# Moving the last tile's projection and key scores beside the gate stage, and spreading its top-k decoding over the expert blocks

## The chip, the core and the metric

The kernel runs on one core of one Trainium2 chip. The metric is the device time of one execution in microseconds (us), lower being better; before the change three executions took 2179.04, 2199.63 and 2200.12 us, with a median of 2199.63. The five engines are named as the profile names them: PE multiplies matrices, DVE and ACT work elementwise on 128 partitions, POOL does elementwise work and issues the indirect DMAs (the gathers), and SP issues the other DMAs, in order, from one queue.

## The reference

One layer of a hybrid decoder: a norm and an input projection, RWKV-7 time mixing and sliding-window attention side by side, an output projection with a residual, and then a PEER layer, to which the change belongs. The prompt has 512 tokens (four tiles of 128), the sample group has 32. Cut to what matters:

```python
def peer(h, lp):                       # 8 heads, 128 keys per half, top 16
    q = (hb @ w_query).reshape(PEER_BLOCK, PEER_HEADS, 2, D_HALF)
    s = jnp.einsum('thcd,cnd->thcn', q, sub_keys)
    s1, i1 = lax.top_k(s[:, :, 0], PEER_TOPK)
    s2, i2 = lax.top_k(s[:, :, 1], PEER_TOPK)
    cand, cidx = ...                   # the 16 x 16 sums, and i1 * 128 + i2
    top, sel = lax.top_k(cand, PEER_TOPK)
    idx = jnp.take_along_axis(cidx, sel, axis=-1)      # 128 experts of a token
    gate = jax.nn.softmax(top, axis=-1)
    act = jax.nn.gelu(jnp.einsum('td,tkd->tk', hb, eu[idx])) * gate
    return jnp.einsum('tk,tkd->td', act, ev[idx])
```

`expert_u` and `expert_v` have 16,384 rows of 1024 float32 each.

## The kernel before

The program is a straight line per engine; a scheduler orders each engine's instructions as the code emits them, by priorities and estimated durations, and every engine then works through its own list in that order.

It has these stages. The front (to about 1110 us) does the projection, the mixing, the attention and the first part of the PEER layer. The experts of the two middle prompt tiles are computed **densely**: the gates of their 256 tokens are spread into a table of 128 x 128 experts, and a loop of 128 blocks multiplies all experts, one block of 128 rows at a time. Those of the first tile, the sample group and the last tile (tile 3) are computed **sparsely**: POOL gathers each token's expert rows with an indirect DMA into a tile `gat`, DVE takes a dot product (`gat<-gat,h` or `gat<-gat,lx`) or adds a weighted row (`x<-gat,act,x`). There are 128 u rows and 128 v rows for a tile, and 32 of each for the sample group. "Rows" of this kind are issued by `beside(n)`, which adds n to a budget and issues one gather with its use per unit; what it takes them from is the list `side`, first in first out. `RATE_G` and `RATE_D` are the budgets of a group of the gates and of a block of the loop.

After the front comes the **gate stage**: two calls of `gates()` (L1387 to L1404) of 16 groups of 8 tokens. In each group DVE compares two one-hot tables (`uH<-vL,aH`, `uL<-vL,aH`), ACT multiplies six of eight by the gate (L1398) and DVE two, PE forms eight 128 x 128 outer products (L1401), and ACT copies them out, to a staging tile `uv` that SP writes to the DRAM tile `gscr` (first call, `stage`), or to `gA` and `gB` (second call, `keep`).

In the **loop** a block loads one block of each table into a tile of tag `uv` (five buffers, `UV`), transposes the u block on PE (L1446), splits both into two fp32r parts (`uH`, `uL`, `vH`, `vL`), multiplies (L1460 to L1463), applies GELU and the gates (`w<-w,gl`, `w<-w,gA`), splits the activation (`aH`, `aL`), and adds into four accumulators (L1477 to L1479). `vL` is a subtraction on POOL (L1453).

The generator `late()` (L1505 to L1551) does tile 3's part of the PEER layer up to its expert numbers: output projection (`w_out`, four steps, PE L1522), norm, transposes, then eight steps of `w_query` (L1544), each product copied (`lq`, L1546), multiplied by the keys (`skT`, L1547) and copied into scores (`lsc`, L1548), and after every second step `two_heads`, which decodes two heads' scores by top-16 searches (`MAX`, `MAX_INDEX`, `MATCH_REPLACE` and small operations on DVE, the `l...` tiles). Only after all eight heads are decoded does it append tile 3's rows to `side`. The loop steps the generator twice a block (`LATE`). The weights of a step are loaded where the step is.

The output stage (L1587 to L1603) adds the accumulators, norms and writes; `beside(1000)` issues whatever rows are left.

Tile pools are stretches of SBUF or PSUM. Where a pool is opened on the bytes of pools that were closed, its first users wait: with the default for every user of the closed pools, with `reuse_waits="tile"` each tile only for the users of what lay on its own bytes.

Of the kernel before, what the change touches and what calls it, by code (L numbers as in the profile page):

```python
# [11 lines left out]
F32 = mybir.dt.float32  # L12
# [5 lines left out]
PSUM = bass.MemoryType.PSUM  # L18
# [16 lines left out]
UV = 5  # L35
AHEAD = 280
RATE_G = 0.8
RATE_D = 3.0
# [75 lines left out]
def hymba_step(ctx, tc, x_prompt, x_sample, cache_k, cache_v, state_wkv, state_shift, meta, norm1_g, w_in, mu, w0,  # L114
# [28 lines left out]
    sscr = dr.tile([32, 16, 128], F32, name="sscr")  # L143
    yscr = dr.tile([128, 8, 128], F32, name="yscr")
# [825 lines left out]
    def two_heads(sc, dst, tile_):  # L970

# [4 lines left out]
        for j in range(4):  # L976
            top16(sc[:, j, :], vals[:, j // 2, j % 2, :], idx[:, j // 2, j % 2, :])
        idf = idx.bitcast(F32)
# [10 lines left out]
        for h in range(2):  # L989
            top16(cand[:, h, :], top[:, h, :], sel[:, h, :])  # L990
        pf = sm()
# [13 lines left out]
        G.tensor_tensor(d1[:, :, 1:16], idf[:, :, 0, 1:16], idf[:, :, 0, 0:15], OP.subtract)  # L1005
        full = [128, 2, 16, 16]
        res = dst[0:2] if len(dst) == 3 else [tile_("res", [128, 32]) for _ in range(2)]
        for r, tab, pos, op, val in ((res[0], first, pf, OP.is_le, d1), (res[1], iota16, bf, OP.is_equal, idf[:, :, 1, :])):
# [3 lines left out]
            V.tensor_reduce(r.rearrange("p (h k) -> p h k", h=2), eq, AX.X, OP.add)  # L1012
        if len(dst) == 2:
            V.scalar_tensor_tensor(dst[0], res[0], 128.0, res[1], OP.mult, OP.add)
# [265 lines left out]
    sb = fr.enter_context(tc.tile_pool(name="sb", bufs=1))  # L1280
    pp = fr.enter_context(tc.tile_pool(name="pp", bufs=1, space=PSUM))
# [98 lines left out]
    def gates(its, sel, ps, put):  # L1380
# [7 lines left out]
        for n, t8 in enumerate(range(0, 128, 8)):  # L1388
# [4 lines left out]
            for q0 in (0, 4):  # L1393
# [8 lines left out]
                put(t8 + q0, p)  # L1402
            with tc.issue_after(marks[-1]):
                beside(RATE_G)  # L1404
# [3 lines left out]
    dn = ctx.enter_context(tc.tile_pool(name="dn", bufs=1))  # L1408
    dp = ctx.enter_context(tc.tile_pool(name="dp", bufs=1, space=PSUM))
# [98 lines left out]
    def late():  # L1508
# [5 lines left out]
        def weights_of(w, n):  # L1514
            wt = dt_("uv", UV, [128, 8, 256])
            DM.dma_start(wt, w[0][:, 256 * n:256 * n + 256].rearrange("(k p) c -> p k c", p=128))
            return wt
        for n in range(4):
            wt = weights_of(w_out, n)
# [17 lines left out]
        for g in range(4):  # L1537
            sc = dt_("lsc", 1, [128, 4, 128])
            for j0 in (0, 2):
                wt = weights_of(w_query, 2 * g + j0 // 2)  # L1540
# [9 lines left out]
            two_heads(sc, [x[:, 32 * g:32 * g + 32] for x in pl1], late_tile)  # L1550
        side.append(tile_experts(3, *pl1, x2))  # L1551
# [8 lines left out]
    gates(its, sels[1], dps, keep)  # L1560
    gl = {}
# [13 lines left out]
    for j in range(128):  # L1575
# [7 lines left out]
        for _ in range(LATE):  # L1583
            next(more, None)
        with tc.issue_after(mark), tc.issue_after(sub):
            beside(RATE_D)
# [45 lines left out]
```

## Time and profile before

| | |
|---|---|
| Runs before (us) | 2179.04, 2199.63, 2200.12; median 2199.63 |
| Profiled execution | 2204.76 us; its span 2203.0 us |
| Busy, share of the span | PE 83%, DVE 77%, POOL 57%, ACT 39% |
| Front | 0 to about 1110 us |
| Gate stage | 1120 to about 1240 us |
| Loop, first to last `aL` | 1245.6 to 2180.3 us |
| After the last block's `aL` | 22.8 us |

All times in the profile are us from the start of the profiled span. The program is the same in each execution; the profiled one lies 5 us above the median of the runs. A row of a timeline is one instruction, or several alike that follow each other ("x6"), with its start and its duration; square brackets give the idle time of the engine before it, and what released it. A row of groups sums the instructions of one line and form. Matmuls are pipelined, and their ends are modelled, so that their starts say more than their durations.

### The profile page before, as it was taken

The page shows a single profiled execution, that of the slowest core. Times are in us where ns is not written, and L with a number is a line of the kernel's source. Part 1 is how long each engine was busy: PE and PEld are TensorE (multiplying, and loading weights), DVE is VectorE, ACT ScalarE, POOL GpSimd, SP SyncE. Part 2 cuts the span into 40 slices and gives each one's busy share as a digit, 9 for nine tenths or more (in the row PEclk, how much of TensorE's full clock was granted, in tenths as well). Part 3 has the DMA queues.
Part 4 walks back from the last instruction along what each step waited for, and adds up shares of the span by engine and source line. Part 5 has one row for each costly group of instructions (what it writes and reads, how often), then busy time and mean ns, then how long its engine had stood idle before and what let it go on. Part 6 is the DMA issues. An engine that isn't in the chain of part 4 may idle for free.

```text
span 2203.0 us, 37197 instructions
## 1 busy us (share of the span) xinstructions
PE 1839.1 (83%) x13915; PEld 1716.0 (78%) x13915; DVE 1690.4 (77%) x3393; ACT 867.3 (39%) x1963; POOL 1249.2 (57%) x963
## 2 busy tenths in 40 slices
PE   5899975585759868996547897899999999999996
PEld 5888974473647747886446787899999999999995
DVE  5543436788788788799989879997778787787887
ACT  6554422211224313323169634334444444444443
POOL 0110103878784676565624546867667776767774
PEclk9999996556755659898778999999999999999998
DMA  7532473687786789996757887799899999999995
GB/s 222 157 101 84 122 191 102 208 288 248 230 273 199 231 273 318 285 317 222 243 163 242 299 313 239 270 326 340 334 330 331 342 326 336 335 325 343 325 330 178
DMA packets 310154, 569.51 MB, mean 259 GB/s; under 512 B 32787, under 2 KB 194565, under 8 KB 309830
## 3 DMA queue, kind: packets, MB, share of 16 engines
q0 software_dynamic: 84048, 305.70, 39.7%
q1 hardware_dynamic: 225926, 261.43, 36.6%
q8 instruction: 110, 1.80, 0.3%
q14 instruction: 70, 0.57, 0.1%
HBM read 543.07 MB, written 24.60 MB: 258 GB/s over the span
## 4 chain that ended last, share of the span: by engine, by line
PE 51%; DVE 22%; DMA 10%; issue 9%; POOL 5%; ACT 3%; SPq 0%; DVEq 0%; POOLq 0%; ACTq 0%
DVE gat L126 5%; PE acc L1478 5%; PE w L1460 5%; PE w L1461 5%; PE w L1463 5%; PE acc L1479 5%; PE acc L1477 5%; PE w L1446 4%; POOL gat L1032 4%; DVE x L126 4%; PE pD L218 3%; DMA gat<-in_expert_v_dram,ei 3%; PE ps L218 2%; DMA wst<-in_w_query_dram 2%; DMA gat<-in_expert_u_dram,ei 2%
## 5 line engine op out<-in xcount | busy, mean ns | idle before, releaser
L126 DVE SCALAR_TENSOR_TENSOR x<-gat,act,x 128x1024 f32<-128x1024 f32 x287 | 427.9, 1491 | 24.7 <-DMA gat<-in_expert_v_dram,ei 23.4
L1032 POOL DMA_INDIRECT gat<-in_expert_u_dram,ei x256 | 343.0, 1340 | 158.8 <-DVE pre L126 75.7
L1032 POOL DMA_INDIRECT gat<-in_expert_v_dram,ei x256 | 294.4, 1150 | 193.6 <-DVE x L126 73.1
L1453 POOL TENSOR_TENSOR vL<-uv,vH 128x1024 fp32r<-128x1024 f32 x128 | 322.5, 2519 | 56.1 <-ACT vH L1452 54.3
L1478 PE MATMUL acc<-aL,vH 128*128 128x256 f32 x1024 | 290.7, 289 | 17.2 <-DVE aL L126 17.1
L1479 PE MATMUL acc<-aH,vL 128*128 128x256 f32 x1024 | 289.3, 287 | 0.0
L1477 PE MATMUL acc<-aH,vH 128*128 128x256 f32 x1024 | 280.5, 295 | 5.3 <-ACT aH L1469 5.3
L1460 PE MATMUL w<-dhH,uH 128*128 128x256 f32 x1024 | 252.5, 284 | 0.2 <-ACT lsc L1548 0.2
L1461 PE MATMUL w<-dhL,uH 128*128 128x256 f32 x1024 | 251.6, 283 | 0.0
L126 DVE CUSTOM_DVE_ANT_0 gat<-gat,h 128x1024 f32<-128x1024 f32 x160 | 213.5, 1343 | 49.6 <-DMA gat<-in_expert_u_dram,ei 47.8
L1478 PEld LDWEIGHTS acc<-aL,vH 128*128 128x128 f32 x1024 | 200.6, 196 | 19.3 <-DVE aL L126 19.3
L126 DVE CUSTOM_DVE_ANT_0 gat<-gat,lx 128x1024 f32<-128x1024 f32 x128 | 214.4, 1686 | 0.0
L1452 ACT CAST vH<-uv 128x1024 fp32r<-128x1024 f32 x128 | 134.6, 1051 | 195.7 <-issue 131.8
L1479 PEld LDWEIGHTS acc<-aH,vL 128*128 128x128 f32 x1024 | 200.6, 196 | 0.0
L1460 PEld LDWEIGHTS w<-dhH,uH 128*128 128x128 f32 x1024 | 196.9, 192 | 0.5 <-ACT lsc L1548 0.4
L1461 PEld LDWEIGHTS w<-dhL,uH 128*128 128x128 f32 x1024 | 196.8, 192 | 0.1
L1477 PEld LDWEIGHTS acc<-aH,vH 128*128 128x128 f32 x1024 | 188.0, 193 | 6.0 <-ACT aH L1469 5.9
L126 DVE TENSOR_TENSOR uL<-w,uH 128x512 fp32r<-128x512 f32 x256 | 167.6, 681 | 3.0 <-ACT uH L1448 3.0
L126 DVE TENSOR_TENSOR w<-w,gl 128x128 f32<-128x128 f32 x128 | 50.5, 395 | 143.3 <-ACT w L1464 143.2
L1463 PE MATMUL w<-dhH,uL 128*128 128x256 f32 x1024 | 151.9, 287 | 2.8 <-DVE uL L126 2.8
L1448 ACT CAST uH<-w 128x512 fp32r<-128x512 f32 x256 | 139.1, 592 | 8.4 <-PE w L1446 3.0
L1446 PE MATMUL w<-ident,uv 128*128 128x128 f32 x1024 | 141.4, 273 | 0.0
(575 smaller groups left out, 4113.8 us busy)
## 6 DMA issues: line engine op xcount, KB each, us to landing
uv<-in_expert_u_dram SPq DMA_DIRECT2D x128, 512.0 KB, 4.5
uv<-in_expert_v_dram SPq DMA_DIRECT2D x128, 512.0 KB, 5.9
wst<-in_w_query_dram SPq DMA_DIRECT2D x48, 512.0 KB, 5.5
wst<-in_w_out_dram SPq DMA_DIRECT2D x24, 512.0 KB, 6.9
wst<-in_w_in_dram SPq DMA_DIRECT2D x20, 512.0 KB, 4.4
h2T<-in_w_in_dram SPq DMA_DIRECT2D x20, 512.0 KB, 4.1
gscr<-uv SPq DMA_DIRECT2D x10, 1024.0 KB, 6.5
gl<-gscr SPq DMA_DIRECT2D x16, 512.0 KB, 7.4
```

What stands on the lines that cost most here:

```text
L126: r = getattr(nc.vector, name)(*args, **kw)
L1032: G.indirect_dma_start(out=r, out_offset=None, in_=w[0], in_offset=bass.IndirectOffsetOnAxis(ap=ei[:, k:k + 1], axis=0))
L1446: T.transpose(p[:, q, :], un[:, 128 * k:128 * k + 128], ident)
L1448: A.copy(uH[:, ks, :], p)
L1452: A.copy(vH, vn)
L1453: G.tensor_tensor(vL, vn, vH.bitcast(F32), OP.subtract)
L1460: T.matmul(pre, uH[:, k, :], hH[:, k, :], start=(k == 0), stop=False)
L1461: T.matmul(pre, uH[:, k, :], hL[:, k, :], start=False, stop=False)
L1463: T.matmul(pre, uL[:, k, :], hH[:, k, :], start=False, stop=(k == 7))
L1477: T.matmul(o, vH[:, ds_], aH, start=(j == 0 and d % 2 == 0), stop=False, skip_group_check=True)
L1478: T.matmul(o, vH[:, ds_], aL, start=False, stop=False, skip_group_check=True)
L1479: T.matmul(o, vL[:, ds_], aH, start=False, stop=(j == 127), skip_group_check=True)
```

## The change

`late()` no longer decodes: it loads its weights one step ahead of their use, writes the scores of every two heads to a DRAM tile `lscr`, and is stepped from inside `gates()`, at every second group (`LATE` = 2). What is left of it is finished before the loop. A new generator, `late_heads()`, reads the scores back and decodes two heads in seven steps (`head_steps`, the old `two_heads` with `yield`s); the loop takes one step per block. Tile 3's rows are appended to `side` after the first two heads, not after all eight. While heads are still to come a block's budget of rows is `RATE_H` = 1.6, later `RATE_D` = 2.4 (3.0 before). Four pools are opened with `reuse_waits="tile"`.

```diff
--- before.py
+++ after.py
@@ -35,7 +35,8 @@
 UV = 5
 AHEAD = 280
 RATE_G = 0.8
-RATE_D = 3.0
+RATE_D = 2.4
+RATE_H = 1.6
 LATE = 2
 GA = 6
 _EARLY = set("m14 pa bt kt AR RW Bn Kn Vn g dx mpa mm".split())
@@ -141,6 +142,7 @@
     hscr_s = dr.tile([32, D], F32, name="hscr_s")
     xscr_s = dr.tile([32, D], F32, name="xscr_s")
     sscr = dr.tile([32, 16, 128], F32, name="sscr")
+    lscr = dr.tile([4, 128, 4, 128], F32, name="lscr")
     yscr = dr.tile([128, 8, 128], F32, name="yscr")
     gscr = dr.tile([16, 128, 128, 8], F32, name="gscr")
     gscr2 = dr.tile([128, 4, 128, 8], F32, name="gscr2")
@@ -968,6 +970,10 @@
                         eq=("ce", 1), res=("res", 2), d1=("d1", 2))[kind], shape, dt)
 
     def two_heads(sc, dst, tile_):
+        for _ in head_steps(sc, dst, tile_):
+            pass
+
+    def head_steps(sc, dst, tile_):
 
 
 
@@ -975,6 +981,8 @@
         vals, idx = tile_("vals", [128, 2, 2, 16]), tile_("idx", [128, 2, 2, 16], U32)
         for j in range(4):
             top16(sc[:, j, :], vals[:, j // 2, j % 2, :], idx[:, j // 2, j % 2, :])
+            if j % 2:
+                yield True
         idf = idx.bitcast(F32)
         V.tensor_copy(idf, idx)
         cand = tile_("cand", [128, 2, 72])
@@ -988,6 +996,7 @@
         top, sel, d1 = tile_("top", [128, 2, 16]), tile_("sel", [128, 2, 16], U32), tile_("d1", [128, 2, 16])
         for h in range(2):
             top16(cand[:, h, :], top[:, h, :], sel[:, h, :])
+        yield True
         pf = sm()
         V.tensor_copy(pf, sel)
         m = sm()
@@ -1003,6 +1012,7 @@
         V.tensor_copy(bf, sel)
         G.tensor_copy(d1[:, :, 0:1], idf[:, :, 0, 0:1])
         G.tensor_tensor(d1[:, :, 1:16], idf[:, :, 0, 1:16], idf[:, :, 0, 0:15], OP.subtract)
+        yield True
         full = [128, 2, 16, 16]
         res = dst[0:2] if len(dst) == 3 else [tile_("res", [128, 32]) for _ in range(2)]
         for r, tab, pos, op, val in ((res[0], first, pf, OP.is_le, d1), (res[1], iota16, bf, OP.is_equal, idf[:, :, 1, :])):
@@ -1010,6 +1020,7 @@
             V.tensor_tensor(eq, bc(tab.unsqueeze(1).unsqueeze(1), full), bc(pos.unsqueeze(3), full), op)
             G.tensor_tensor(eq, eq, bc(val.unsqueeze(2), full), OP.mult)
             V.tensor_reduce(r.rearrange("p (h k) -> p h k", h=2), eq, AX.X, OP.add)
+            yield True
         if len(dst) == 2:
             V.scalar_tensor_tensor(dst[0], res[0], 128.0, res[1], OP.mult, OP.add)
         gate = dst[-1].rearrange("p (a b) -> p a b", a=2)
@@ -1277,8 +1288,8 @@
             project(blk, wt, ws, jps(), lambda k: [t[:, k, :] for t in hA], NA, _t(pj, "own", 2, [128, NA]),
                     _t(pj, "po", 3, [128, NA]), 0)
 
-    sb = fr.enter_context(tc.tile_pool(name="sb", bufs=1))
-    pp = fr.enter_context(tc.tile_pool(name="pp", bufs=1, space=PSUM))
+    sb = fr.enter_context(tc.tile_pool(name="sb", bufs=1, reuse_waits="tile"))
+    pp = fr.enter_context(tc.tile_pool(name="pp", bufs=1, space=PSUM, reuse_waits="tile"))
     def meta_wkv():
         r = rwkv_prep(40, 16)
         wkv_local(r)
@@ -1400,13 +1411,15 @@
                         V.tensor_scalar(o1[:, q, :], iot, i2T[:, t], gaT[:, t], OP.is_equal, OP.mult)
                     T.matmul(p[:, 128 * (q - q0):128 * (q - q0) + 128], o0[:, q, :], o1[:, q, :], start=True, stop=True)
                 put(t8 + q0, p)
+            if n % LATE:
+                next(more, None)
             with tc.issue_after(marks[-1]):
                 beside(RATE_G)
 
 
     ND = 256
-    dn = ctx.enter_context(tc.tile_pool(name="dn", bufs=1))
-    dp = ctx.enter_context(tc.tile_pool(name="dp", bufs=1, space=PSUM))
+    dn = ctx.enter_context(tc.tile_pool(name="dn", bufs=1, reuse_waits="tile"))
+    dp = ctx.enter_context(tc.tile_pool(name="dp", bufs=1, space=PSUM, reuse_waits="tile"))
 
     def dt_(tag, bufs, shape, dt=F32):
         return _t(dn, tag, bufs, shape, dt)
@@ -1511,12 +1524,19 @@
         yT = dt_("ly", 1, [128, 8, 128])
         DM.dma_start(yT, yscr)
 
-        def weights_of(w, n):
-            wt = dt_("uv", UV, [128, 8, 256])
-            DM.dma_start(wt, w[0][:, 256 * n:256 * n + 256].rearrange("(k p) c -> p k c", p=128))
-            return wt
+        todo = [(w_out, n) for n in range(4)] + [(w_query, n) for n in range(8)]
+        ready = []
+
+        def weights_of():
+
+            while todo and len(ready) < 2:
+                w, n = todo.pop(0)
+                wt = dt_("uv", UV, [128, 8, 256])
+                DM.dma_start(wt, w[0][:, 256 * n:256 * n + 256].rearrange("(k p) c -> p k c", p=128))
+                ready.append(wt)
+            return ready.pop(0)
         for n in range(4):
-            wt = weights_of(w_out, n)
+            wt = weights_of()
             p = dps()[:, 0:256]
             for k in range(8):
                 T.matmul(p, yT[:, k, :], wt[:, k, :], start=(k == 0), stop=(k == 7))
@@ -1535,9 +1555,9 @@
         h_transposed(x2, 128, put, dps)
         yield True
         for g in range(4):
-            sc = dt_("lsc", 1, [128, 4, 128])
+            sc = dt_("gl", 2, [128, 4, 128])
             for j0 in (0, 2):
-                wt = weights_of(w_query, 2 * g + j0 // 2)
+                wt = weights_of()
                 for j in range(2):
                     p = dps()
                     for k in range(8):
@@ -1547,8 +1567,21 @@
                     T.matmul(p[:, 128:256], qT, skT[:, j, :], start=True, stop=True)
                     A.copy(sc[:, j0 + j, :], p[:, 128:256])
                 yield True
-            two_heads(sc, [x[:, 32 * g:32 * g + 32] for x in pl1], late_tile)
-        side.append(tile_experts(3, *pl1, x2))
+            DM.dma_start(lscr[g], sc)
+        held[:] = [x2]
+
+    coming = [True]
+
+    def late_heads():
+
+        for g in range(4):
+            if g == 1:
+                side.append(tile_experts(3, *pl1, held[0]))
+            sc = dt_("lsc", 1, [128, 4, 128])
+            DM.dma_start(sc, lscr[g])
+            yield from head_steps(sc, [x[:, 32 * g:32 * g + 32] for x in pl1], late_tile)
+            yield True
+        coming[0] = False
 
     for n in range(AHEAD):
         with tc.issue_after(marks[gather_mark[0]]):
@@ -1558,6 +1591,9 @@
     sels = [sel_transposed(0, dps, dt_("selT", 1, [128, 3, 128])), sel_transposed(1, dps, dt_("lsc", 1, [128, 3, 128]))]
     gates(its, sels[0], dps, stage)
     gates(its, sels[1], dps, keep)
+    for _ in more:
+        pass
+    more = late_heads()
     gl = {}
 
     def gate_of(j):
@@ -1580,10 +1616,9 @@
             ins[j + 2], sub = block_in(j + 2)
         block_v(j, mid)
         mid = nxt
-        for _ in range(LATE):
-            next(more, None)
+        next(more, None)
         with tc.issue_after(mark), tc.issue_after(sub):
-            beside(RATE_D)
+            beside(RATE_H if coming[0] else RATE_D)
     oT = gB[:, 0:16, :].rearrange("p a b -> p (a b)").rearrange("p (a b) -> p a b", b=ND)
     for c in range(4):
         A.copy(oT[:, 2 * c:2 * c + 2, :], acc[c])
```

The first place is SP's queue from the start of the gates on; `lx` and `ly` are inputs of `late()`, `gscr<-uv` the first half's gate writes. Before:

```order
L1510 DMA lx_10045<-in_x_prompt_dram 128x1024
L1512 DMA ly_10047<-yscr 128x1024
L1490 DMA gscr<-uv_8934 128x16x128
L1490 DMA gscr<-uv_8989 128x16x128
L1490 DMA gscr<-uv_9047 128x16x128
L1490 DMA gscr<-uv_9102 128x16x128
L1490 DMA gscr<-uv_9160 128x16x128
L1490 DMA gscr<-uv_9218 128x16x128
L1490 DMA gscr<-uv_9273 128x16x128
```

and now:

```order
L1523 DMA lx_8973<-in_x_prompt_dram 128x1024
L1525 DMA ly_8975<-yscr 128x1024
L1535 DMA uv_8977<-in_w_out_dram 128x8x256
L1535 DMA uv_8979<-in_w_out_dram 128x8x256
L1503 DMA gscr<-uv_8935 128x16x128
L1535 DMA uv_9049<-in_w_out_dram 128x8x256
L1503 DMA gscr<-uv_9008 128x16x128
L1535 DMA uv_9119<-in_w_out_dram 128x8x256
L1503 DMA gscr<-uv_9078 128x16x128
L1535 DMA uv_9186<-in_w_query_dram 128x8x256
L1503 DMA gscr<-uv_9145 128x16x128
L1547 DMA uv_9256<-in_norm_g_dram 128x1024
```

The weight loads, which stood behind the first block's tables, now stand between the gate writes, one of them behind each.

The second place is DVE in blocks 1 and 2 of the loop as changed: `w<-w,gl` and `w<-w,gA` are a block's gate products, `uL` its halves, `l...` tiles the decoding, `x<-gat,act,x` a row of the sample group.

```order
L127 TENSOR_TENSOR leq_10757<-first,lsm_10654 128x512
L127 SCALAR_TENSOR_TENSOR x_2114_9374<-gat_10197,act_9371,x_2114_9374 128x1024
L127 RECIPROCAL sR_10936<-sR_10935 128x2
L127 TENSOR_TENSOR lsm_10656<-lsm_10656,lsm_10658 128x32
L127 TENSOR_TENSOR w_10379<-w_10379,gl_10246 128x128
L127 TENSOR_TENSOR ga_12_107<-ga_12_107,sR_10936 128x32
L127 TENSOR_TENSOR lsm_10656<-lsm_10656,lsm_10661 128x32
L127 TENSOR_TENSOR w_10379<-w_10379,gA_8038 128x128
L127 TENSOR_SCALAR lsm_10664<-lsm_10656 128x32
L127 TENSOR_TENSOR uL_10415<-w_10416,uH_10414 128x512
L127 TENSOR_TENSOR lsel_10557<-lsel_10557,lsm_10664 128x32
L127 TENSOR_TENSOR uL_10415<-w_10423,uH_10414 128x512
```

Before, the decoding stood between the `aL` of the fifth block and that of the 15th; now 27 of its 196 instructions stand ahead of the first `aL`, and the other 169 between the first and the 15th.

The third place is DVE at the end, from the last block's gate product on (`x<-gat,act,x`: tile 3's rows, `uv<-uv,w`: the residual of the dense tiles). Before:

```order
L126 TENSOR_TENSOR w_21431<-w_21431,gA_14387 128x128
L126 SCALAR_TENSOR_TENSOR x_3022_15006<-gat_18627,act_15003,x_3022_15006 128x1024
L126 TENSOR_TENSOR aL_21460<-w_21431,aH_21459 128x256
L126 SCALAR_TENSOR_TENSOR x_3022_15006<-gat_18709,act_15003,x_3022_15006 128x1024
L126 SCALAR_TENSOR_TENSOR x_3022_15006<-gat_18712,act_15003,x_3022_15006 128x1024
L126 SCALAR_TENSOR_TENSOR x_3022_15006<-gat_18715,act_15003,x_3022_15006 128x1024
```

and now:

```order
L127 SCALAR_TENSOR_TENSOR x_3228_16603<-gat_20403,act_16600,x_3228_16603 128x1024
L127 TENSOR_TENSOR w_21444<-w_21444,gA_14265 128x128
L127 SCALAR_TENSOR_TENSOR x_3228_16603<-gat_20406,act_16600,x_3228_16603 128x1024
L127 TENSOR_TENSOR aL_21473<-w_21444,aH_21472 128x256
L127 SCALAR_TENSOR_TENSOR x_3228_16603<-gat_20488,act_16600,x_3228_16603 128x1024
L127 SCALAR_TENSOR_TENSOR x_3228_16603<-gat_20491,act_16600,x_3228_16603 128x1024
L127 SCALAR_TENSOR_TENSOR x_3228_16603<-gat_20494,act_16600,x_3228_16603 128x1024
L127 TENSOR_TENSOR uv_21530<-uv_21530,w_21532 128x512
L127 TENSOR_TENSOR uv_21558<-uv_21558,w_21560 128x512
L127 SCALAR_TENSOR_TENSOR x_3228_16603<-gat_20576,act_16600,x_3228_16603 128x1024
L127 TENSOR_TENSOR uv_21530<-uv_21530,w_21538 128x512
L127 TENSOR_TENSOR uv_21558<-uv_21558,w_21566 128x512
```

Behind the last `aL` three rows stood before, and 22 stand now; 26 gathers stand behind the last `vL` on POOL where three stood. Tile 3's first row is used behind the eighth `aL` of the program before, and behind the 15th of the one changed: the rows of the sample group are ahead of it in `side`.

## Rows read from the trace of the kernel before

**Rows 1.** Windows by stage: busy us of each engine, then clock, DMA share.

```profile
1124.00:1190.00 66.00, 45.95 (x292) 42.30 (x293) 63.89 (x99) 61.48 (x160) 22.59 (x15) 0.85 0.77 230
...
1304.00:1436.00 132.00, 110.28 (x868) 107.31 (x867) 127.61 (x361) 53.28 (x104) 90.26 (x77) 0.95 0.75 259
...
1480.00:2148.00 668.00, 668.00 (x5653) 668.00 (x5653) 530.77 (x801) 281.12 (x507) 483.93 (x307) 1.00 0.92 333
```

**Rows 2.** DVE timeline: start, us; `aL` of blocks 0, 5, 16, 22, 127.

```profile
1245.63 0.42 DVE L126 TENSOR_TENSOR aL<-w,aH 128x256 fp32r<-128x256 f32 x1 [0.49 <-ACT aH L1469]
...
1304.34 0.40 DVE L126 TENSOR_TENSOR aL<-w,aH 128x256 fp32r<-128x256 f32 x1
...
1435.57 0.41 DVE L126 TENSOR_TENSOR aL<-w,aH 128x256 fp32r<-128x256 f32 x1
...
1480.33 0.42 DVE L126 TENSOR_TENSOR aL<-w,aH 128x256 fp32r<-128x256 f32 x1 [0.49 <-ACT aH L1469]
...
2180.25 0.41 DVE L126 TENSOR_TENSOR aL<-w,aH 128x256 fp32r<-128x256 f32 x1
```

**Rows 3.** DVE timeline in the gates: starts of two groups.

```profile
1129.20 1.94 DVE L126 TENSOR_TENSOR uH<-vL,aH 128x1024 f32<-128x1024 bf16 x1
...
1235.05 1.90 DVE L126 TENSOR_TENSOR uH<-vL,aH 128x1024 f32<-128x1024 bf16 x1
```

**Rows 4.** Groups by line, 1250 to 1482 us: busy, mean ns, idle before.

```profile
L1544 PE MATMUL w<-ly,uv 128*128 128x128 f32 x256 | 32.4, 284 | 6.4 <-DVE uL L126 4.6 <-ACT lsc L1548 1.8
...
L1522 PE MATMUL w<-uv,ly 128*128 128x256 f32 x64 | 14.1, 379 | 0.0
...
L1547 PE MATMUL w<-skT,lq 128*128 128x128 f32 x32 | 6.3, 281 | 0.0
...
L1548 ACT COPY lsc<-w 128x128 f32<-128x128 f32 x16 | 4.1, 264 | 15.3 <-PE w L1547 10.5 <-DVE lidx L126 4.8
```

**Rows 5.** Groups by line on PE, 1124 to 1240 us.

```profile
L1401 PE MATMUL w<-vH,uH 128*128 128x128 f32 x512 | 78.6, 315 | 41.2 <-ACT vH L1398 25.4 <-DVE uH L126 15.4
```

**Rows 6.** ACT timeline in the second half of the gates.

```profile
1194.34 2.25 ACT L1398 ACTIVATE vH<-uL,lsc 128x128 f32<-128x128 bf16 x6
...
1206.02 0.24 ACT L1498 COPY gA<-w 128x128 f32<-128x128 f32 x1
...
1206.59 1.19 ACT L1398 ACTIVATE vH<-uL,lsc 128x128 f32<-128x128 bf16 x3
```

**Rows 7.** Timeline of DVE, SP and PE where the gates begin.

```profile
1109.94 0.69 DVE L126 TENSOR_REDUCE dsel<-ce 128x32 f32<-128x512 f32 x1 [1.44 <-POOL ce L1011]
...
1110.69 0.82 SPq L1421 DMA_DIRECT2D uv<-hscr  x2
...
1114.57 3.65 PE L1426 MATMUL w<-ident,uv 128*128 128x128 f32 x16 [33.62 <-DMA uv<-hscr]
...
1120.24 1.89 DVE L126 TENSOR_TENSOR uH<-vL,aH 128x1024 f32<-128x1024 bf16 x1
```

**Rows 8.** Windows of tile `gat` alone, columns as in Rows 1.

```profile
1304.00:1436.00 132.00, 0.00 (x0) 0.00 (x0) 56.17 (x33) 1.15 (x2) 37.85 (x32) 0.95 0.75 259
...
1480.00:2148.00 668.00, 0.00 (x0) 0.00 (x0) 322.62 (x205) 0.00 (x0) 232.96 (x205) 1.00 0.92 333
```

**Rows 9.** DVE timeline: the last expert row.

```profile
2186.76 1.28 DVE L126 SCALAR_TENSOR_TENSOR x<-gat,act,x 128x1024 f32<-128x1024 f32 x1 [0.93 <-DMA gat<-in_expert_v_dram,ei]
```

**Rows 10.** DVE timeline in the front: two expert rows, 22 rows apart.

```profile
731.26 1.28 DVE L126 SCALAR_TENSOR_TENSOR x<-gat,act,x 128x1024 f32<-128x1024 f32 x1
...
768.96 1.28 DVE L126 SCALAR_TENSOR_TENSOR x<-gat,act,x 128x1024 f32<-128x1024 f32 x1 [0.60 <-DMA gat<-in_expert_v_dram,ei]
```

**Rows 11.** DMA issues: KB each, median us to landing.

```profile
uv<-in_w_out_dram SPq DMA_DIRECT2D x4, 1024.0 KB, 8.8
```

**Rows 12.** Timeline of DVE and POOL at one moment of the loop.

```profile
2136.21 3.55 DVE L126 SCALAR_TENSOR_TENSOR x<-gat,act,x 128x1024 f32<-128x1024 f32 x1
...
2136.27 2.40 POOL L1453 TENSOR_TENSOR vL<-uv,vH 128x1024 fp32r<-128x1024 f32 x1
```

## The prediction, made before the changed kernel had run

> **What bounds the kernel now.** I read the windows by stage first, then DVE's timeline at the borders of the stages and blocks, then groups and single rows where a term needed a price.
>
> The gate stage is bound by DVE: it is busy 63.89 of 66 us, ACT 61.48, PE only 45.95 at a granted clock of 0.85, so at the lower of its two levels (1.2 and 2.4 GHz) for part of the time [rows 1]. One group follows the other in (1235.05 − 1129.20) / 29 = 3.65 us [rows 3], a pair in 7.3. PE has room there, some 2.4 us a pair: sixteen groups' products at 78.6 / 32 = 2.46 us a group make 4.9 of 7.3 [rows 5].
>
> The loop is bound by PE in its long part: 668 of 668 us at clock 1.00 between 1480 and 2148, DVE 531 [rows 1]. From the 23rd block's `aL` to the 128th's, 105 blocks take 2180.25 − 1480.33 = 699.92 us, 6.667 each [rows 2]. All 127 intervals at that pace would be 846.7; they take 934.6. The excess of **88 us** lies in the first 22 intervals. Part of it is PE's work for tile 3: 32.4 + 14.1 + 6.3 = 52.8 us [rows 4]. The rest is DVE: between 1304 and 1436 it is busy 127.61 of 132 us and PE 110.28 [rows 1], and 11 blocks pass there, 12 us each [rows 2].
>
> At the end, 2203.0 − 2180.25 = 22.75 us lie behind the last `aL`, of which the last row, 2186.76 [rows 9], and what follows it are 16.2.
>
> **The change part by part.** The sums are made against the profiled execution, 2204.8 us; it lies 5.1 above the median of 2199.6, and the difference is then taken off the median.
>
> *Border to the gates.* PE stands idle 33.62 us, until the loads of `hscr`, issued at 1110.69 right behind the front's last DVE operation at 1109.94, have landed and been transposed; the first gate group starts at 1120.24 [rows 7]. With the pools' finer waits these loads wait for older users only, and the transposes (3.65) can be done before 1110. Only the selection's transposes are left behind the last reduction: the gates begin near 1114, **−6** (0 to −8). At the front's own pools I take 0: SP still waits for the same writes there.
>
> *Gates.* Added: four `w_out` steps, a norm with transposes, eight `w_query` steps, one a pair.
> - `w_out` and the two `w_query` steps of the first half: PE needs 4.9 + 14.1 / 4 = 8.4 us a pair instead of DVE's 7.3: 6 × 1.1 = 7.
> - Norm: two DVE passes over 128x1024 at some 1.28 (that of an expert row [rows 9]) and eight transposes at 3.65 / 16 [rows 7], 4.4 us, with their hand-overs 5.
> - Six `w_query` steps in the second half: ACT needs for a half group's six multiplications 2.25 per six and 0.57 per three copies [rows 6], for a pair 12 × 0.375 + 4 × 0.57 = 6.8; four copies at 0.264 [rows 4] make it 7.9, and PE's multiplication by the keys waits for a copy that stands between them, some 0.3 more: 8.2 against 7.3, 6 × 0.9 = 5; with the queueing of a copy behind up to six multiplications (2.25) once in a pair where the order is worst, 8.
>
> Sum **+20**. Bounds: +6, where only DVE's added passes count, and +53, where no product finds room. I take 20, nearer to the lower end, for PE's idle share in the stage is a third.
>
> *Block 0.* Twenty search operations of the first heads stand ahead of the first block's gate product; at 48.5 / 181 = 0.27 each (below) 5.4 us, half of it beside PE: **+3**.
>
> *Loop.* The products are gone; what stays is DVE. Its own work is (530.77 − 322.62) / 100.2 = 2.08 us a block [rows 1, 8], an expert row 56.17 / 33 = 1.70 [rows 8], and decoding with the end of the sample group 127.61 − 56.17 − 11 × 2.08 = 48.5 us for 181 decoding instructions [rows 1, 8]. In the changed order the first 14 intervals hold 169 of these (45.3), 18 rows (30.6) and 14 × 2.08 = 29.1: 105 us, at the 97% of rows 1's middle window 108. PE wants 14 × 6.667 = 93.3. So DVE still sets the pace there, by 15 us; with what spills into the next blocks the excess is 18 (5 if the order packs well, 45 if the searches, a chain each, block the split of `uL` that PE waits for). 88 − 18: **−70** (−43 to −83). Later a block has 2.4 rows, 2.08 + 2.4 × 1.57 (the mean of [rows 8]) = 5.9 us, below PE's 6.67.
>
> *Tail.* The rows of tile 3 begin seven blocks later, and 22 instead of 3 are left behind the last `aL`. This is the cover that is lost: 19 rows that ran free beside PE now run alone. The nearest price is that of rows in the front, 22 in 768.96 − 731.26 = 37.7 us, 1.71 each [rows 10]; the dearest is that of the loop, 668 / 205 = 3.26 [rows 8]; the cheapest DVE's own 1.28 [rows 9]. 37.7 and some 14 for the last norm and write make 51.7 against 22.75: **+29** (+20 to +63).
>
> Sum: −6 + 20 + 3 − 70 + 29 = **−24**: 2180.8 on the profiled scale, **2176** on the median's. Within its own bounds this case reaches from 2156 to 2196.
>
> **The rivals.**
>
> A, the forecast, −24: 0.46. One per cent, 22 us, is about what a measurement of this kernel can tell from no change, and A's middle lies near it: 0.27 of it counts as faster, 0.19 as same.
>
> D, both prices at their better ends: the products fit PE's gaps (+6 for +20) and the tail's rows run at 1.38 us, near DVE's own (−7): −45, **2155**. For it speaks PE's third of idle time in the gates; against it that DVE and ACT are both above 93% there [rows 1]. 0.13, faster.
>
> B, nothing of the products is hidden in the gates (+53): +9, **2209**. ACT's share of 93% speaks for it. 0.12, same.
>
> C, the port that POOL and DVE share. Where a row of DVE ran beside a `vL` of POOL it took 3.55 us for 1.28, 2.27 more [rows 12]. If that befalls one row or search in each of the first 14 blocks, where DVE sets the pace, it costs 14 × 2.27 = 32 us, of which some 8 are in the 1.70 already: +24, **2200**. 0.07, same. The Trainium skill ("SBUF — State Buffer", Who interferes with whom) says that a VectorE instruction with two inputs in SBUF and a GpSimd instruction that reads SBUF exclude each other for the whole instruction; by that rule C would be certain for every row and for none of the one-input searches, and the trace agrees as far as that one row.
>
> F, the tail's rows go at the loop's 3.26: 22 × 1.55 = +34 on A, **2210**. Against it: that pace was set by PE and the budget, not by the gathers. 0.06, same. Here the change doesn't do what it says, rows from the first heads on, since the sample group's rows go first.
>
> E, slower: **weights come late**. Each weight load stands in SP's queue behind a gate write that waits for its own pair's last copy. That leaves a load about a pair and a half, 12 us, and the median landing of such a load was 8.8 [rows 11]. The DMA share in the gates is 0.77 already [rows 1], and twelve such loads more come in there. From 12 us on PE's next product waits, and behind it, in order, the gate products, then ACT's copies and DVE's staging tiles. At twice the landing, some 17 us, each of 12 loads lengthens its pair by 4: +48 on A, **2224**. 0.14.
>
> Rest 0.02, slower (a wait that I don't see).
>
> **How the numbers follow.** The predicted time is A's, 2176. Faster by over 1%: 0.27 + 0.13 = 0.40. Within 1%: 0.19 + 0.12 + 0.07 + 0.06 = 0.44. Slower: 0.16. The range from 2152 to 2214 takes in A with its bounds, B, C and F, and most of D; left out are D's better half (0.05) and E with the rest, 0.16 at the most, of which a landing of 15 us would still fall inside.
>
> **What would show it.** Right: the first gate group near 1114; a pair of groups in 8 to 8.5 us; the first `aL` some 17 us later than 1245.63; the first 14 intervals of `aL` in 105 to 115 us, then 6.67 each; 22 rows behind the last `aL`, taking 35 to 40 us. Wrong: PE's matmuls of `w_out` or `w_query` released by their weights' DMA (E); pairs at 7.5 (D) or above 10 us (B); rows of 3.5 us beside each `vL` in the first 14 blocks (C); rows of the tail more than 2 us apart (F). If the blocks right after the decoding stay above 7 us, the budget of 2.4 rows is too much for DVE, and the loop's term is wrong.

## The result, and the profile after

The changed kernel takes 2181.34 us against 2199.84 (medians), a ratio of 0.9914 with an interval of 0.9888 to 0.9941: 18.5 us less. The forecast was 24 less, 2176. The interval leaves out 1, so the gain is clear of noise; at 0.9% it lies just under the one per cent by which the prediction divided its chances.

The profiled execution has a span of 2179.0 us, 24.0 under that of before, but not only in the way that was forecast. Four borders split it:

| Stage | before | after | difference | forecast |
|---|---|---|---|---|
| Front, to the start of its last reduction | 1109.9 | 1103.0 | −6.9 | 0 |
| Last reduction to first gate group | 10.3 | 3.6 | −6.7 | −6 |
| First gate group to first `aL` | 125.4 | 144.7 | +19.3 | +23 |
| First to last `aL` | 934.6 | 878.5 | −56.1 | −70 |
| Behind the last `aL` | 22.8 | 49.2 | +26.4 | +29 |

The front's 6.9 us can't be put down to the change: in twelve profiles whose fronts have the same instructions and waits, the last reduction lies anywhere from 1098.8 to 1119.7. I therefore compare profiles **from the start of that reduction to the end of the span**, 1093.1 us before and 1076.0 after: **−17.1**, which fits the medians' −18.5. That the whole span fell by exactly the forecast's 24 is chance.

The border, on DVE, PE and SP (start, duration; answers to [rows 7]):

```profile
1103.01 0.69 DVE L127 TENSOR_REDUCE dsel<-ce 128x32 f32<-128x512 f32 x1 [1.44 <-POOL ce L1021]
...
1106.63 1.89 DVE L127 TENSOR_TENSOR uH<-vL,aH 128x1024 f32<-128x1024 bf16 x1
...
1104.35 0.90 PE L1379 MATMUL w<-ident,dsel 128*128 128x128 f32 x3 [20.18 <-DVE dhL L127]
...
1073.86 1.07 SPq L1434 DMA_DIRECT2D uv<-hscr  x2
```

SP issues the `hscr` loads 29 us ahead of the last reduction instead of right behind it, and only the selection's transposes are left on PE.

The gates on PE, by line (x: count, then busy us and mean ns, then idle time before), and two DVE rows six pairs of groups apart (answers to [rows 3 to 5]):

```profile
L1564 PE MATMUL w<-ly,uv 128*128 128x128 f32 x256 | 31.9, 278 | 0.0
L1542 PE MATMUL w<-uv,ly 128*128 128x256 f32 x64 | 14.5, 380 | 0.3 <-ACT vH L1409 0.3
```

```profile
1183.27 1.99 DVE L127 TENSOR_TENSOR uH<-vL,aH 128x1024 f32<-128x1024 bf16 x1
...
1230.98 1.96 DVE L127 TENSOR_TENSOR uH<-vL,aH 128x1024 f32<-128x1024 bf16 x1
```

The products run without waiting for a weight. A pair takes 47.71 / 6 = 7.95 us, where 8.2 was forecast. What sets its pace is PE (the same window, columns as in [rows 1]):

```profile
1183.27:1230.98 47.71, 47.71 (x409) 46.29 (x408) 45.74 (x59) 45.18 (x168) 20.11 (x11) 1.00 0.95 330
```

PE is busy throughout, at a granted clock of 1.00; its products there start 0.11 us apart, and nowhere more than 0.28. DVE and ACT each have some 2 us to spare.

The loop: `aL` of blocks 0, 14, 22 and 127 (answers to [rows 2]), then the windows by stage of blocks 0 to 14 and of the tail (columns as in [rows 1]).

```profile
1251.30 0.41 DVE L127 TENSOR_TENSOR aL<-w,aH 128x256 fp32r<-128x256 f32 x1
...
1370.67 0.41 DVE L127 TENSOR_TENSOR aL<-w,aH 128x256 fp32r<-128x256 f32 x1
...
1426.25 0.42 DVE L127 TENSOR_TENSOR aL<-w,aH 128x256 fp32r<-128x256 f32 x1
...
2129.82 0.41 DVE L127 TENSOR_TENSOR aL<-w,aH 128x256 fp32r<-128x256 f32 x1
```

```profile
1251.00:1371.00 120.00, 101.86 (x770) 97.72 (x768) 116.43 (x321) 50.34 (x84) 67.55 (x61) 0.91 0.60 206
...
2129.00:2179.00 50.00, 6.63 (x40) 6.19 (x40) 35.66 (x34) 11.51 (x30) 25.12 (x21) 0.58 0.75 261
```

The first 14 intervals take 119.4 us (105 to 115 expected), with DVE busy 116.43 of 120; the next eight take 55.6, and the last 105 take 703.6, 6.70 each. The clearest rows of the first stretch are those where DVE and POOL meet (answer to [rows 12]), DVE's first:

```profile
1256.69 4.81 DVE L127 SCALAR_TENSOR_TENSOR x<-gat,act,x 128x1024 f32<-128x1024 f32 x1
...
1265.98 2.64 DVE L127 CAST lsm<-lsel 128x32 f32<-128x32 uint32 x1
```

```profile
1256.76 2.40 POOL L1466 TENSOR_TENSOR vL<-uv,vH 128x1024 fp32r<-128x1024 f32 x1
1259.09 1.31 POOL L1021 TENSOR_TENSOR leq<-leq,ld 128x512 f32<-128x512 f32 x1
...
1266.17 2.40 POOL L1466 TENSOR_TENSOR vL<-uv,vH 128x1024 fp32r<-128x1024 f32 x1
```

A row of 1.28 us takes 4.81 while POOL does `vL` and then a decoding product. Even a CAST of 32 columns takes 2.64 beside a `vL`, where it takes 0.18 with nothing beside it. Of the 18 rows of that form, nine met an elementwise instruction of POOL and took 2.53 us on average; nine met none and took 1.27. The searches keep their time: a MAX8 over 128x128 takes 0.28 us in either case. And POOL waits too: a `vL` that finds one of DVE's additions under way takes 3.39 us.

The tail on DVE (answer to [rows 9]):

```profile
2153.32 1.28 DVE L127 SCALAR_TENSOR_TENSOR x<-gat,act,x 128x1024 f32<-128x1024 f32 x1 [2.14 <-DMA gat<-in_expert_v_dram,ei]
2155.06 6.57 DVE L127 SCALAR_TENSOR_TENSOR x<-gat,act,x 128x1024 f32<-128x1024 f32 x5 [0.46 <-DMA gat<-in_expert_v_dram,ei]
...
2169.61 1.29 DVE L127 SCALAR_TENSOR_TENSOR x<-gat,act,x 128x1024 f32<-128x1024 f32 x1 [0.98 <-DMA gat<-in_expert_v_dram,ei]
```

Twenty-two rows end at 2170.9: 41.1 us, 1.87 each, with waits for gathers between them and the dense tiles' last norm among them.

### The profile page after: what moved, and what is told of

Read it like the earlier page. It is cut to its first block, busy times and chain, and to the rows that moved or that the text cites. A ratio compares the mean times of both kernels' runs of the same rounds, so it can differ in the third digit from the quotient of the medians.

```text
span 2179.0 us, 37214 instructions
## 1 busy us (share of the span) xinstructions
PE 1839.2 (84%) x13915; PEld 1713.9 (79%) x13915; DVE 1667.8 (77%) x3393; ACT 863.5 (40%) x1962; POOL 1232.3 (57%) x963
## 4 chain that ended last, share of the span: by engine, by line
PE 52%; DVE 19%; DMA 11%; issue 9%; POOL 5%; ACT 4%; SPq 0%; POOLq 0%; DVEq 0%; ACTq 0%
PE acc L1491 5%; PE acc L1492 5%; PE w L1473 5%; PE w L1474 5%; PE acc L1490 4%; PE w L1476 4%; POOL gat L1043 4%; PE w L1459 4%; DVE x L127 4%; PE pD L220 3%; DVE gat L127 3%; DMA gat<-in_expert_u_dram,ei 3%; DMA gat<-in_expert_v_dram,ei 3%; DMA wst<-in_w_query_dram 2%; PE pD L954 2%
## 5 line engine op out<-in xcount | busy, mean ns | idle before, releaser
L127 DVE SCALAR_TENSOR_TENSOR x<-gat,act,x 128x1024 f32<-128x1024 f32 x287 | 437.2, 1523 | 24.9 <-DMA gat<-in_expert_v_dram,ei 22.4
L1043 POOL DMA_INDIRECT gat<-in_expert_u_dram,ei x256 | 323.1, 1262 | 173.7 <-DVE pre L127 81.7
L1043 POOL DMA_INDIRECT gat<-in_expert_v_dram,ei x256 | 304.5, 1189 | 190.8 <-DVE x L127 78.9
L1466 POOL TENSOR_TENSOR vL<-uv,vH 128x1024 fp32r<-128x1024 f32 x128 | 317.4, 2480 | 60.1 <-ACT vH L1465 57.9
L127 DVE CUSTOM_DVE_ANT_0 gat<-gat,lx 128x1024 f32<-128x1024 f32 x128 | 175.7, 1384 | 7.4 <-DMA gat<-in_expert_u_dram,ei 7.4
```

Of the source, the lines that this page charges most:

```text
L127: r = getattr(nc.vector, name)(*args, **kw)
L1043: G.indirect_dma_start(out=r, out_offset=None, in_=w[0], in_offset=bass.IndirectOffsetOnAxis(ap=ei[:, k:k + 1], axis=0))
L1466: G.tensor_tensor(vL, vn, vH.bitcast(F32), OP.subtract)
```

## The experiments

Median and ratio are of the timed runs, against the kernel before; the other columns are from one profile each, in us: last reduction to end of span, first gate group to first `aL`, intervals 1 to 14 of `aL`, 15 to 22, 23 to 127, and what lies behind the last `aL`. A ratio is against executions of the kernel before made along with that kernel (their medians lie between 2195.8 and 2201.9), so that ratios compare better than medians. Only three intervals lie clear of the change's: finer waits alone, no low part, and no load ahead. Smaller differences from the change rest on the parts of single profiles. Two kernels with the same loop, the change and no load ahead, differ by 1.2 us in the first 22 intervals, 175.0 and 173.8.

| Kernel | median | ratio (interval) | red. to end | gates | 1–14 | 15–22 | 23–127 | tail |
|---|---|---|---|---|---|---|---|---|
| before | 2199.84 | | 1093.1 | 125.4 | 175.3 | 59.4 | 699.9 | 22.8 |
| change | 2181.34 | 0.9914 (0.9888–0.9941) | 1076.0 | 144.7 | 119.4 | 55.6 | 703.6 | 49.2 |
| finer waits alone | 2191.27 | 0.9985 (0.9954–1.0017) | 1086.6 | 127.0 | 174.7 | 59.5 | 699.9 | 21.8 |
| decoding at once | 2174.80 | 0.9883 (0.9842–0.9924) | 1066.5 | 144.3 | 126.0 | 56.3 | 701.2 | 35.0 |
| no low part | 2162.01 | 0.9829 (0.9782–0.9876) | 1058.4 | 144.3 | 107.3 | 49.5 | 703.6 | 50.1 |
| budget 2.4 | 2181.79 | 0.9928 (0.9904–0.9953) | 1073.3 | 144.7 | 134.9 | 55.2 | 699.5 | 35.4 |
| low part on DVE | 2181.65 | 0.9920 (0.9882–0.9958) | 1073.6 | 145.0 | 116.9 | 57.1 | 702.1 | 48.8 |
| low part in quarters | 2170.68 | 0.9875 (0.9807–0.9943) | 1065.9 | 145.2 | 111.9 | 53.4 | 702.4 | 49.4 |
| no load ahead | 2213.53 | 1.0058 (1.0022–1.0094) | 1106.3 | 176.1 | 120.3 | 53.5 | 703.6 | 49.2 |
| at once, low part on DVE | 2171.35 | 0.9883 (0.9812–0.9954) | 1064.4 | 145.2 | 137.1 | 59.2 | 701.5 | 17.8 |
| at once, quarters | 2165.89 | 0.9861 (0.9816–0.9905) | 1068.7 | 144.1 | 123.5 | 54.3 | 707.6 | 35.5 |
| budget 2.4, quarters | 2178.01 | 0.9896 (0.9861–0.9931) | 1068.4 | 144.4 | 125.4 | 54.1 | 705.6 | 35.2 |
| at once, all in quarters | 2189.39 | 0.9962 (0.9930–0.9993) | 1084.9 | 144.5 | 122.8 | 53.5 | 722.8 | 37.7 |

**The finer waits alone**, in the kernel before:

```diff
-    dn = ctx.enter_context(tc.tile_pool(name="dn", bufs=1))
+    dn = ctx.enter_context(tc.tile_pool(name="dn", bufs=1, reuse_waits="tile"))
 # the same for dp, sb, pp
```

> The kernel before with the finer waits of the four pools alone. The profile of the changed kernel has two gains there: 6.7 us between the front's last reduction and the first gate group (10.3 us before, 3.6 after), and 6.9 us within the front, which I had not forecast. Theory 1: only the border is the waits' doing, the front's 6.9 us is the spread between executions: border 3.6 us, the last reduction near 1110, median some 6 us under before, 2193. Theory 2: both are: the last reduction near 1103, some 13 us under before, 2186. Nothing else moves: first to last aL 934 us as before.

```profile
1103.94 0.69 DVE L126 TENSOR_REDUCE dsel<-ce 128x32 f32<-128x512 f32 x1 [1.44 <-POOL ce L1011]
...
1107.57 1.89 DVE L126 TENSOR_TENSOR uH<-vL,aH 128x1024 f32<-128x1024 bf16 x1
```

The border is 3.6 us as in the change, and everything behind it is as before: −6.5 from the reduction on. Its own reduction is as early as the change's, which spoke for theory 2; the later profiles, with 1098.8 to 1119.7 for the same front, and the ratio speak for theory 1: the interval reaches from 10 us less to 4 us more, which holds theory 1's 6 us and leaves out theory 2's 13. What the front itself gained, up to some 4 us, stays open: there is only one profile of the front before, 1109.9, beside twelve that spread over 21 us.

**Decoding at once**: two heads in one piece a block, tile 3's rows behind all eight, budget 3.0.

```diff
-RATE_D = 2.4
-RATE_H = 1.6
+RATE_D = 3.0
+RATE_H = 3.0
 # cut: in late_heads(), in the loop over g
-            if g == 1:
-                side.append(tile_experts(3, *pl1, held[0]))
 # cut
-            yield from head_steps(sc, [x[:, 32 * g:32 * g + 32] for x in pl1], late_tile)
+            two_heads(sc, [x[:, 32 * g:32 * g + 32] for x in pl1], late_tile)
             yield True
+        side.append(tile_experts(3, *pl1, held[0]))
```

> The changed kernel with two heads decoded in one piece, a piece a block, tile 3's rows only after all eight heads, and the budget of rows 3.0 throughout, as before; the products stay beside the gates. 14 rows are left behind the last aL instead of 22. Theory 1, spreading matters since PE waits behind bunched searches: the first 14 intervals of aL take over 140 us (119 in the change), the tail 8 x 1.87 = 15 us less, together slower than the change by 5 to 20 us: 2186 to 2200. Theory 2, DVE's sum of work decides, not its order: the tail gives back what the loop loses, 2176 to 2184.

The loop is 5 us longer and the tail 14 shorter, with eight rows fewer in it. Theory 1 falls; theory 2 is the nearer one, with a median just below its range. From the reduction on the profile is even 9.5 us better than the change's, but the timed intervals overlap. No gain from spreading the decoding and starting the rows earlier shows here.

Set beside the finer waits alone, this kernel shows what the moved products are worth: both have the budget of before and tile 3's rows behind all eight heads, and apart from the pace of the decoding they differ in where the products stand, with their loads one step ahead. From the reduction on it is 20.1 us less (1066.5 against 1086.6), and the two ratios' intervals do not overlap. So the products beside the gates carry the gain of the change.

**No low part** of the first 18 blocks (that part of the result is left out):

```diff
-        G.tensor_tensor(vL, vn, vH.bitcast(F32), OP.subtract)
+        if j < 18:
+            G.memset(vL.bitcast(F32), 0.0)
+        else:
+            G.tensor_tensor(vL, vn, vH.bitcast(F32), OP.subtract)
```

> The changed kernel with the low part vL of the first 18 blocks left out: POOL writes zeros there and reads nothing. Theory 1, DVE stands still while POOL reads for vL (2.4 us a block), in the stretch where DVE sets the pace: the first 14 intervals of aL shrink from 119 us to about 100, rows there take 1.3 to 1.5 us instead of 1.90, and the median is 15 to 25 us under the change, 2156 to 2166. Theory 2, DVE simply has that much work of its own: 115 to 120 us, the time of the change, 2181.

Groups of DVE in the first 14 intervals, of the change and then of this kernel:

```profile
L127 DVE SCALAR_TENSOR_TENSOR x<-gat,act,x 128x1024 f32<-128x1024 f32 x18 | 34.2, 1899 | 0.0
...
L127 DVE CAST lsm<-lsel 128x32 f32<-128x32 uint32 x8 | 5.1, 636 | 0.0
```

```profile
L127 DVE SCALAR_TENSOR_TENSOR x<-gat,act,x 128x1024 f32<-128x1024 f32 x18 | 23.6, 1312 | 0.0
...
L127 DVE CAST lsm<-lsel 128x32 f32<-128x32 uint32 x8 | 2.5, 313 | 0.0
```

Theory 1: the same 18 rows take 1.31 instead of 1.90 us, and the 22 intervals 18.2 us less. The zeros also leave POOL more time, so that a rival would be that its results come sooner; but DVE's busy time in the first 14 intervals falls from 115.9 to 99.2 us, with two more rows in them, so DVE's own instructions got shorter. POOL's reading cost DVE that much, in the stretch where DVE sets the pace.

**Budget 2.4** (`RATE_H = 2.4`):

> The changed kernel with the budget of rows at 2.4 while heads are to come (1.6 in the change): 12 rows behind the last aL instead of 22, the tail 10 x 1.87 = 19 us shorter (30 us). Theory 1, where DVE sets the pace every row costs its own time: the first 22 intervals grow from 175 us by up to 10 x 1.9 = 19, and the sum is the change's, 2178 to 2184. Theory 2, part of the rows finds room in blocks 14 to 30, where DVE is 83% busy: 8 to 15 us faster than the change, 2166 to 2173.

Ten rows left the tail (−13.8) and entered the first 14 intervals (+15.5). Theory 1: a row costs 1.4 to 1.6 us in either place.

**Low part on DVE** (`V.tensor_tensor` in the first 18 blocks):

> The changed kernel with the subtraction for vL of the first 18 blocks on DVE instead of POOL. Without it the first 22 intervals were 18 us shorter. On DVE it should take about 1.28 us (a row's time), 18 x 1.28 = 23 us. Theory 1, only DVE's time counts there: 23 - 18 = 5 us slower than the change, 2183 to 2190, rows at 1.3 us each. Theory 2, POOL, freed of 18 x 2.4 us, brings rows earlier and DVE's stops were longer than the rows show: faster than the change, 2165 to 2176.

The subtraction takes 1.21 us on DVE and rows fall to 1.36; the loop's sum is 2.4 us less, the time the change's. Neither theory's time came; nearest is the first, with gain and price about equal.

**Low part in quarters**, first 18 blocks:

```diff
+        for c in range(4 if j < 18 else 1):
+            x = slice(256 * c, 256 * c + 256) if j < 18 else slice(0, D)
+            G.tensor_tensor(vL[:, x], vn[:, x], vH[:, x].bitcast(F32), OP.subtract)
```

> The changed kernel with the same subtraction of the first 18 blocks on POOL as four pieces of 256 columns. Theory 1, a DVE instruction that meets one of POOL stands for the whole rest of that instruction: with pieces of some 0.7 us rows there fall from 1.90 to about 1.5 us, the first 14 intervals from 119 to about 110, the time to 2170 to 2175. Theory 2, POOL's sum of reading is taken from DVE, however it is cut: rows stay at 1.8 to 1.9 and the time at 2178 to 2184.

The 22 intervals are 9.7 us shorter, and from the reduction on it is 10.1 less than the change; the timed intervals of the two overlap. The rows take 1.60 us, which alone proves little, for with no load ahead, where the loop is the change's, the same 18 took 1.53: which instruction meets POOL differs from profile to profile. The sums speak for theory 1: a DVE instruction stands for the rest of the POOL instruction that it meets, so shorter ones cost less. It does not hold for every row:

```profile
1260.28 5.21 DVE L127 SCALAR_TENSOR_TENSOR x<-gat,act,x 128x1024 f32<-128x1024 f32 x1
1260.34 2.82 POOL L1468 TENSOR_TENSOR vL<-uv,vH 128x256 fp32r<-128x256 f32 x4
1263.12 1.28 POOL L1021 TENSOR_TENSOR leq<-leq,ld 128x512 f32<-128x512 f32 x1
```

This one stood for all four pieces and for the decoding product behind them.

**No load ahead** (`len(ready) < 1`):

> The changed kernel with each weight loaded where its step is, not one step ahead. Theory 1, the load ahead is what keeps PE from waiting: each of 12 steps waits for a part of a landing of 6 to 9 us, PE's L1542 and L1564 show idle time ended by that DMA, first gate group to first aL 145 us grow by 20 to 40: 2200 to 2220. Theory 2, the order of SP's queue already issues the loads early enough, or the steps have slack: 2179 to 2186.

PE by line in the gates:

```profile
L1564 PE MATMUL w<-ly,uv 128*128 128x128 f32 x256 | 35.8, 304 | 10.6 <-DMA uv<-in_w_query_dram 10.6
...
L1542 PE MATMUL w<-uv,ly 128*128 128x256 f32 x64 | 19.5, 473 | 14.5 <-DMA uv<-in_w_out_dram 14.5
```

Theory 1: 25.1 us of waits for weights, and 31.4 us more between the first gate group and the first `aL`. Without the load one step ahead the change is slower than the kernel before.

**At once, low part on DVE**:

> The decoding in one piece a block, budget 3.0 (2174.8 us), with the low parts of the first 18 blocks on DVE: no row is left behind the last aL (14 there, 22 in the change), the second ten blocks have 35 rows (20 there). Theory 1, a row costs DVE the same 1.3 us in the tail and in the blocks where DVE sets the pace: the tail some 13 us shorter, the first 22 intervals 15 rows and 23 us of low parts less 18 us of stops longer, 2175 to 2185. Theory 2, rows in the blocks after the decoding find room beside PE: 2160 to 2170, the fastest of all.

No row is left for the tail (17.8 us), but the first 22 intervals take 196.3. Against decoding at once: tail −17.2, intervals +14.0, so that 2 us are left. That is theory 1's exchange, though the intervals grew by less than the 24 us that its terms add up to; the median, 2171, lies between the two ranges.

**At once, quarters; budget 2.4, quarters; at once, all 128 blocks in quarters:** the loop over quarters as above, in the first 24 blocks (`j < 24`) or in all; "at once" with the edit of decoding at once, "budget 2.4" with `RATE_H = 2.4`.

> The decoding in one piece a block with budget 3.0 (2174.8 us in its own run, 27 us from the front's last reduction to the end less than the kernel before) and the low parts of the first 24 blocks in four pieces each (10 us less in the changed kernel). Theory 1, the two gains add: 35 to 38 us less than before from the last reduction on, ratio 0.982 to 0.985, some 2163. Theory 2, both shorten the same waits: no more than the better of the two, ratio 0.987 to 0.989, 2171.

> The change's spread decoding with budget 2.4 and the low parts of the first 24 blocks in four pieces: the same 13 rows behind the last aL as the version that decodes two heads in one piece a block, so that the two differ in the spreading of the decoding alone. Theory 1, spreading is worth nothing where DVE sets the pace: both within 4 us of each other, 2161 to 2167. Theory 2, spreading saves PE's waits behind bunched searches: this one is 5 to 10 us faster, 2155 to 2160.

> As the version with decoding in one piece and low parts in four pieces, but in all 128 blocks. Theory 1, behind block 22 PE sets the pace and DVE's stops cost nothing: the same time within 3 us, rows there fall from 1.52 to about 1.35 us each. Theory 2, some of PE's waits there come from DVE's stops: the last 105 intervals fall below 700 us, by up to 5.

The first two differ in the spreading, and in the code also in the budget (3.0 and 2.4) and in where tile 3's rows are appended; but both have the same number of rows in each stretch (27, 16 and 218, and 13 in the tail). From the reduction on they take 1068.7 and 1068.4 us. So these profiles show no worth of spreading, as the first theory of the second text had it; the medians differ by 12, with intervals that overlap, and the second one's, 2178, lies outside both of its ranges. The gains of the first did not add: its first 22 intervals are 4.5 us better than with whole low parts, and its last 105 are 6.4 worse. The second shows the same against budget 2.4 (705.6 for 699.5). Both lose it right behind the blocks with pieces: from the `aL` of block 22 to that of block 30 they take 59.6 for 50.4 us, and 57.1 for 49.8. Why stays open. The first one's ratio is the lowest of the kernels that compute everything, but its interval overlaps the change's. In all blocks the pieces do harm, against both theories: the intervals of this kernel's ratio and of the first one's do not overlap. POOL in the last 105 intervals, of this kernel and then of the change:

```profile
L1469 POOL TENSOR_TENSOR vL<-uv,vH 128x256 fp32r<-128x256 f32 x421 | 411.7, 1007 | 1.9
```

```profile
L1466 POOL TENSOR_TENSOR vL<-uv,vH 128x1024 fp32r<-128x1024 f32 x105 | 259.9, 2475 | 43.8 <-ACT vH L1465 41.8
```

Four pieces make 3.9 us a block instead of 2.5, and the intervals there grow from 703.6 to 722.8. POOL is then busy for 663.9 of 715 us of that stretch, 93%, against 72% in the change. That it has become the limit there is likely, but was not tried.

## Why the prediction was right, and which of its steps failed

- *Border, −6*: measured −6.7, and alone in the first experiment −6.5. Right.
- *Gates and block 0, +23*: +19.3, made of two misses that partly cancel. Between the first and the last group's start it is +11.8, where +20 was forecast; between the last group and the first `aL` it is +7.4, where block 0 was to cost 3. The norm, priced at 5, leaves one gap of 9.93 us between two groups (1158.26 to 1168.19), 6 over the usual, of which DVE waits 2.2 for the sample group's activation. The pairs of the second half took 7.95 us for 8.2, but not as ACT's sum, which is how I had got the 8.2: PE, which was to have room, worked without a pause. My own [rows 4] price a `w_query` step at (32.4 + 6.3) / 8 = 4.8 us on PE, with the gate products 9.7 a pair; I priced two of these steps like `w_out`'s, at 3.5, and the other six by ACT alone. It came to no more than 7.95 at a granted clock of 1.00, where the kernel before had 0.88 (1194 to 1231 us). That the price was near is luck. That the 7.4 are ACT's backlog of copies, and block 0's product behind the searches, is read from order and times, not tried.
- *Loop, −70*: −56.1. This is the step that was mis-sized. I had 105 us of DVE's work in the first 14 intervals and 108 for their time; they took 119.4. Counting each of DVE's instructions up to the start of the next, the blocks' own work took 28.5 us for 29.1, the decoding 47.0 for 45.3, the 18 rows 32.8 for 30.6, and the last sums of the sample group (`h<-h,x`, `h<-h,gat`) 7.6, for which the sum has no term: the 48.5 us that I called decoding with the end of the sample group are the decoding's alone, and most of these sums stand in the 56.17 of tile `gat` and were spread over its 33 "rows". That omission is the larger part of the 10.8 us by which DVE's work came out above my sum. The other thing that I had too small are the stops behind POOL, which are inside these figures: without POOL's reads the decoding took 39.8 us, 20 rows 24.5, and the 14 intervals 107.3. So rival C's mechanism was at work inside case A, at 18 us for 22 blocks rather than the 32 for 14 that I priced, of which I had thought 8 were counted. The last 105 intervals added 3.7 us that I had not forecast; the kernel with budget 2.4 does not show them (699.5). The Trainium skill's rule ("SBUF — State Buffer", Who interferes with whom) was right on the rows: those that met POOL took 2.53 us, the others 1.27. The same section of the Trainium skill says that a cast, too, can contend with GpSimd. The 128x32 CAST of 2.64 us beside a `vL` agrees. I had let only two-input operations count; that the searches go free, I had right.
- *Tail, +29*: +26.4, again two misses that cancel: 22 rows took 41.1 us for 37.7, with the dense tiles' end among them, and what follows them 8.1 for some 14.
- *Rival E*, late weights: its wait exists (25 us of it) and is kept off by the load one step ahead; the change's SP queue left the loads early enough.
- *The 2.4 rows a block* did not bind: the order holds some 2.1 a block, and the intervals behind block 22 took 6.70 us.
- *The case's own bounds*, 2156 to 2196, are not the sum of the terms' bounds, which would reach some 18 us further down and 80 further up; they were a judgement.

Where the gain went: of the 88 us excess, 56 came back, and 18 of the 32 that stayed are POOL's reads. Of the 56, 26 are paid again in the tail, where the rows that left the early blocks run alone, and 19 in the gates.

## What to carry to other kernels

Work that moves from an engine-bound stretch to another place is worth its price there: here ten rows cost 1.6 us each in the early blocks and 1.4 in the tail, so that shifting rows or spreading the decoding earned nothing that could be seen, while moving products into PE's idle time in the gates did. When such room is filled, price the engine that had it: in the second half of the gates PE then set the pace. Where DVE sets the pace, look for its long instructions and at what POOL reads at that moment; cutting POOL's instruction shortened that stretch here, and cutting it in every block lengthened the rest. Compare profiles from a border behind which only the change differs: a front of the same instructions varied here by 21 us.

## What the runs showed of the hardware

- DVE instructions stood up to 3.5 us behind POOL's elementwise reads (4.81 for 1.28), one-input casts too (2.64 for 0.18); searches did not (0.28 us). POOL's subtraction, 2.40 us, took up to 3.39 when DVE's instruction had come first.
- A subtraction on POOL cut in four took 4 × 0.98 = 3.9 us instead of 2.48 beside a busy DVE: half of the pieces took under 0.75 us, the slowest 1.82.
